# Where keys are normalized and how attention is spread over the projections: a diffusion block on one core

## The chip, the cores and the metric

The kernel runs on one core of one Trainium2 chip. The metric is the device time of one execution in microseconds (us), as the median of several runs. Five engines work side by side, each through its own queue in order: TensorE (PE, matmuls and transposes), VectorE (DVE), ScalarE (ACT), GpSimd (POOL) and SyncE (SP, which issues the DMAs here). Lower is better.

## The reference, cut to what matters

One layer of a transformer block: adaLN from a condition vector, neighbourhood attention over 256 latent tokens and 256 context tokens with 16 heads of 128, and a gated ConvFFN. All in float32.

```python
def project(t):
    q, k, v = jnp.split(t @ w_qkv, 3, axis=-1)
    sh = (t.shape[0], t.shape[1], NA_HEADS, HEAD_DIM)
    return rms_norm(q.reshape(sh), q_g), rms_norm(k.reshape(sh), k_g), v.reshape(sh)

sh1, sc1, g1, sh2, sc2, g2 = adaln(cond_lat, w_ada[i], b_ada[i])
h = modulate(rms_norm(x, norm_mix_g[i]), sh1, sc1)
hc = modulate(rms_norm(ctx, norm_mix_g[i]), csh1, csc1)
q, k, v = project(h)
qc, kc, vc = project(hc)
# per block of 128 queries: scores against 256 latent keys (with a bias and a window) and 256 context keys
p = jax.nn.softmax(jnp.concatenate([s_lat, s_ctx], axis=-1), axis=-1)
o = einsum(p[..., :nk], vb) + einsum(p[..., nk:], vc)
x = x + g1 * (o @ w_o)
hf = modulate(rms_norm(x, norm_ffn_g[i]), sh2, sc2)
x = x + g2 * conv_ffn(hf, ...)
```

What matters here: queries and keys of each head are normalized over the head's 128 features (`rms_norm` with `q_g`, `k_g`), after the projection and before the scores.

## The kernel before, in words

**Split matmuls.** Float32 precision is made of two reduced-precision halves (`F32R`). Each weight tile of 256 x 512 is loaded by SP (`wload`, line 133), ACT casts its high half (`wh`, line 155), and DVE subtracts it from the original for the low half (`wl`, line 156). `ahead` (line 180) makes these pairs two tiles ahead of their use. Activations have high and low halves as well (`hh`, `hl`). A projection (`project`, line 383) adds three products for each weight tile and each tile of 128 tokens (`nat`, lines 378 to 380): six matmuls of 512 columns for one token tile and one weight tile.

**Passes.** The heads are worked in four groups of four (512 columns). A projection pass runs over eight weight tiles; a K or V pass has four token tiles (latent and context tokens), a Q pass two (latent alone). The products of the first K and of V for groups 0 and 1 run ahead, beside the modulation of the input (`first_products`). Then comes a Q pass for group 0, and for g = 0, 1, 2: (V of group 2 when g is 1), K of group g+1, Q of group g+1. After these V of group 3 is projected, then the output projection (`proj` with `w_o`), then the FFN, which fills the span from about 718 us on.

**Side work.** While group g+1 is projected, group g's attention runs in between. It is cut into pieces in a list, `side`; after each token tile of each weight tile `nat` adds `side.rate` to a credit, and each whole credit runs the next piece (line 381). A piece of attention is a score S (three matmuls, bias, maximum, exponential, scaling by the row's sum, line 600), a turn T (four transposes of the probabilities and their split into halves, line 627), or a weighing W (twelve matmuls with V, line 641). A head has two S, two T and one W. The order before is S0 S0 T0 T0 S1 S1 T1 T1 W0 S2 S2 W1 T2 T2 S3 S3 W2 T3 T3 W3, the number being the head's. A second list, `ada`, computes the modulation vectors g1, sh2 and gs2: 12 columns of 8 pieces each and one last piece, 97. Each piece loads 512 KB of `w_ada` (`wa`, three buffers); three pieces of eight multiply and add on DVE (line 279), five multiply on ACT (line 276) and add on POOL (line 277). It is ticked once per weight tile, by 0.44 times the token tiles (line 387).

**Normalization before.** After K and Q of the next group are projected and copied out of PSUM (`out_of_psum`, line 678), the side list is drained, and then `split_k` and `split_q` run `norm_transpose` (line 515) for four and two token tiles. It squares each of the four heads on ACT with an accumulated sum (line 521), forms the mean, takes the inverse root with a power on POOL and one Newton step on DVE (`rsqrt_newton`, lines 195 to 200), multiplies into a new tile `qn` (line 526), transposes it head by head on PE (line 532), and writes the high half with ACT (line 534) and the low half with DVE (line 535). The rows of probabilities, `qn` and some others share three buffers of one tag (`row2k`).

**Who orders the work.** The program is traced in this order, and a scheduler then settles the order of each engine's queue from planned durations: an instruction that stands earlier in the program has precedence among those that are ready, and scores are given a higher precedence. On the chip each engine runs its queue in that order and waits where an operand is late.

Of the kernel before, what the change touches and what calls it, by code (L numbers as in the profile page):

```python
# [15 lines left out]
P = 128  # L16
# [9 lines left out]
CH = 512  # L26
KT = 2

RATE, RATE3 = 0.46, 0.36

WA = 3
EPS = 1e-6
# [18 lines left out]
def block_kernel(  # L51
# [20 lines left out]
    def pj():  # L72
        return ps.tile([P, CH], F32, tag="pj", name="pj", bufs=4)
# [9 lines left out]
    def at():  # L83

        turns.append(0)
        return (ms, mx)[len(turns) % 2]()
# [39 lines left out]


    NDR, REP = 7, 66
    rp = cp.tile([NH * NDR, 31], F32, name="rp")
    nc.scalar.dma_start(rp, rpb)  # L130


    def wload(src, k0, kn, c0, cn, pool=None):
# [201 lines left out]

    xctx = ExitStack()
    xp = xctx.enter_context(tc.tile_pool(name="xp", bufs=1))
    s32 = xp.tile([P, KD, 32], F32, name="s32")
    nc.vector.memset(s32, 0.0)
    nc.scalar.copy(s32[:, :, 0:2], sT)  # L340
# [29 lines left out]
    def nat(psl, tt0, w, kt0, n, first, last):  # L370

        wh, wl = w
        for i, pt in enumerate(psl):
            ts = slice((tt0 + i) * P, (tt0 + i + 1) * P)
            for k in range(n):
                kt = kt0 + k
                a, z = first and k == 0, last and k == n - 1
                nc.tensor.matmul(pt, hh[:, kt, ts], wh[:, k, :], start=a, stop=False)  # L378
                nc.tensor.matmul(pt, hh[:, kt, ts], wl[:, k, :], start=False, stop=False)  # L379
                nc.tensor.matmul(pt, hl(kt, ts), wh[:, k, :], start=False, stop=z)  # L380
# [129 lines left out]
    ap = actx.enter_context(tc.tile_pool(name="ap", bufs=1))  # L510

    def row2k(name):
        return ap.tile([P, CH], F32, tag="r2", name=name, bufs=3)

    def norm_transpose(pt, gcol, dh, dl, t0):

        ss = ap.tile([P, 4], F32, tag="ss", name="ss", bufs=2)
        qn = row2k("qn")
        for h in range(4):
            hc = slice(h * HD, (h + 1) * HD)  # L520
            nc.scalar.activation(qn[:, hc], pt[:, hc], AF.Square, accum_out=ss[:, h : h + 1])
# [4 lines left out]
        nc.vector.tensor_tensor(  # L526
            out=qn.rearrange("p (h d) -> p h d", d=HD), in0=pt.rearrange("p (h d) -> p h d", d=HD),
            in1=r.unsqueeze(2).to_broadcast([P, 4, HD]), op=ALU.mult,
        )
        tp = at()  # L530
        for h in range(4):
            nc.tensor.transpose(tp[:, h * P : (h + 1) * P], qn[:, h * HD : (h + 1) * HD], ident)
        tpv = tp.rearrange("p (h t) -> p h t", t=P)
        nc.scalar.activation(dh[:, :, t0 : t0 + P], tpv, AF.Copy, scale=gcol)
        nc.vector.scalar_tensor_tensor(
            out=dl[:, :, t0 : t0 + P], in0=tpv, scalar=gcol,
            in1=dh[:, :, t0 : t0 + P].bitcast(F32), op0=ALU.mult, op1=ALU.subtract,
        )

    def split_k(kps):  # L540
        kh = kv.tile([P, 4, 2 * T], F32R, tag="kh", name="kh")
        kl = kv.tile([P, 4, 2 * T], F32R, tag="kl", name="kl")
        for tt in range(4):
            norm_transpose(kps[tt], kg, kh, kl, tt * P)
        return kh, kl

    def split_q(qps):
        qq = kv.tile([P, 2, 4, T], F32R, tag="qq", name="qq")
        qh, ql = qq[:, 0], qq[:, 1]
        for tt in range(2):  # L550
            norm_transpose(qps[tt], qg, qh, ql, tt * P)
        return qh, ql
# [36 lines left out]

    def attention(g, q, k, v):  # L590

        (qh, ql), (kh, kl) = q, k

        bank = lambda: ms() if late else at()

        def head(h4):
# [3 lines left out]
            def scores(qt):  # L600
                with tc.high_priority():
                    if qt == 0:
                        if h + 1 < NH:
                            bias(h + 1)
                        st["bt"] = biases.pop(h)
                        st["ph"] = kv.tile([P, 4, T], F32R, tag="pth", name="pth", bufs=2)
                        st["pl"] = ap.tile([P, 4, T], F32R, tag="ptl", name="ptl", bufs=2)
# [11 lines left out]
                    nc.vector.tensor_reduce(out=nm, in_=sp, axis=AX.X, op=ALU.max, negate=True)  # L619
# [4 lines left out]
                    nc.scalar.mul(pr, pr, rs)  # L624
                    st[qt] = pr

            def turn(qt):
                tq = slice(qt * P, (qt + 1) * P)
                pr, tp = st[qt], ms()
                for kt in range(4):  # L630
                    nc.tensor.transpose(
                        tp[:, kt * P : (kt + 1) * P], pr[:, kt * P : (kt + 1) * P], ident
# [23 lines left out]

            return scores, turn, weigh

        heads = [head(h4) for h4 in range(4)]
        s = [[lambda f=h[0], t=t: f(t) for t in range(2)] for h in heads]  # L660
        t = [[lambda f=h[1], t=t: f(t) for t in range(2)] for h in heads]
        w = [[h[2]] for h in heads]
# [5 lines left out]
    cols = [ada_tasks(ap, 2, c, g1T) for c in range(4)]  # L668
    cols += [ada_tasks(ap, 3, c, sh2T) for c in range(4)]
    cols += [ada_tasks(ap, 4, c, gs2T, S_GF) for c in range(4)]  # L670
# [3 lines left out]
    kw, qw = [  # L674
        oT[:, a : a + 2 * n, :].rearrange("p (t a) c -> p t (a c)", t=n) for a, n in ((8, 4), (4, 2))
    ]

    def out_of_psum(pts, dst):

        for tt, pt in enumerate(pts):  # L680
            nc.scalar.copy(dst[:, tt, :], pt)
        return [dst[:, tt, :] for tt in range(len(pts))]

    k = split_k(out_of_psum(kps, kw))
    q = split_q(out_of_psum(project(0, 2), qw))
    for g in range(3):
        side.extend(sum(attention(g, q, k, v), []))
        c0 = (g + 1) * CH
        side.rate = RATE3 if g == 1 else RATE
        if g == 1:  # L690
            v = [split_v(project(2 * D + c0, 4), g + 1)]
        if g == 2:
            kq = big.tile([P, 6, CH], F32, tag="row1", name="kq")
            kw, qw = kq[:, :4], kq[:, 4:]
# [9 lines left out]
    v = []  # L704
    early, rest = attention(3, q, k, v)
# [45 lines left out]
    sacc2 = ap.tile([P, T], F32, name="sacc2")  # L751
    tail = [sacc2]

    def omv(kt, c):
        return om[0][:, kt, c]
# [7 lines left out]
    for i, pieces in enumerate(WO):  # L763
# [3 lines left out]
        elif i > 1:  # L767
            pts = {c: [bank() for _ in range(cn // P)] for c, cn, _, _ in pieces}
        for c, cn, k_lo, k_hi in pieces:
            tick = (lambda: side.tick(cn / 340)) if i == 0 else (lambda: ada.tick(1.0))  # L770
            proj(w_o, NH, c, cn, omv, tick, k_lo, k_hi, pts[c], fold)
        if i == 0:
            side.drain()
            continue
        if i == len(WO) - 2:
            ada.drain()
# [182 lines left out]
```

## Time and profile before

| what | value |
|---|---|
| median of 3 runs | 1447.01 us (1440.1 to 1449.32) |
| the profiled execution's own time | 1445.85 us |
| its span, first to last instruction | 1444.0 us |
| granted TensorE clock, mean | 0.992 |
| PE / DVE / ACT / POOL busy | 1399.1 / 1000.0 / 778.5 / 281.1 us |
| HBM read | 312.75 MB, 219 GB/s over the span |

Busy time is the sum over an engine's instructions without their overlap; matmuls are pipelined, so a new one starts every 0.23 us while one of 512 columns is shown as lasting 0.39. A row of a group names the line, engine, operation, tiles written and read, shapes and count, then busy us and mean ns of one, then the engine's idle time just before and what ended it. A row of a window has each engine's busy us (and its number of instructions), the granted clock as a share, the DMA engines' share and GB/s. A row of waits has the total, the number of times and the longest. A row of a line's own view has minimum, median and maximum ns, and the first and last start.

### The profile page before, as it was taken

To read this page: it belongs to the slowest core of one execution; us is meant where nothing else is said; L and a number is where in the kernel's file an instruction comes from. 1 tells how busy PE (TensorE), PEld (TensorE's weight loads), DVE (VectorE), ACT (ScalarE), POOL (GpSimd) and SP (SyncE) were. 2 spreads that over 40 slices of the span, in tenths; PEclk is the share of its full clock that TensorE was granted. 3 is DMA by queue.
4 is the path that set the end of the run, shared out by engine and by line. 5 is a ranking of instruction groups with operands and counts; after the bars stand their busy time and mean duration, and the time that the engine had idled before them with its cause. 6 is when DMAs were issued, how large, how long until landed. Compare 5 with 4: busy or idle time off the path is not lost.

```text
span 1444.0 us, 21091 instructions
## 1 busy us (share of the span) xinstructions
PE 1399.1 (97%) x7608; PEld 1167.8 (81%) x7608; DVE 1000.0 (69%) x1541; ACT 778.5 (54%) x1356; POOL 281.1 (19%) x208
## 2 busy tenths in 40 slices
PE   5999999999999999999899999999999999999998
PEld 2666787877787887888788888888888888888888
DVE  4556687686868768756768787887877775545454
ACT  4322265775555675755556566665666654333333
POOL 1000025465445555300101111111111000000000
PEclk9999999999999999999899999999999999999999
DMA  9999548687677677545567777777776666566554
GB/s 308 357 333 313 190 125 269 206 259 218 214 219 254 215 239 232 178 138 189 174 201 224 237 230 242 236 229 234 228 240 196 182 175 206 182 207 204 172 173 156
DMA packets 208920, 317.14 MB, mean 220 GB/s; under 512 B 23360, under 2 KB 87744, under 8 KB 208816
## 3 DMA queue, kind: packets, MB, share of 16 engines
q1 hardware_dynamic: 208688, 315.79, 70.4%
q8 instruction: 59, 0.97, 0.3%
q14 instruction: 45, 0.37, 0.1%
q10 hardware_dynamic: 128, 0.01, 0.0%
HBM read 312.75 MB, written 3.01 MB: 219 GB/s over the span
## 4 chain that ended last, share of the span: by engine, by line
PE 74%; issue 9%; DMA 5%; DVE 4%; ACT 3%; POOL 2%; SPq 1%; DVEq 0%; POOLq 0%; ACTq 0%
PE pj L727 18%; PE pj L733 9%; PE mx L727 8%; PE ms L727 7%; PE pj L379 5%; PE pj L378 5%; PE pj L380 5%; PE mx L733 4%; PE ms L733 4%; DMA wa<-in_w_ada 3%; PE ms L411 2%; PE mx L378 2%; PE mx L379 2%; PE mx L380 2%; POOL acc L277 2%
## 5 line engine op out<-in xcount | busy, mean ns | idle before, releaser
L156 DVE TENSOR_TENSOR wl<-wr,wh 128x1024 fp32r<-128x1024 f32 (+2 forms) x425 | 503.8, 1186 | 280.6 <-PE pj L733 106.3
L155 ACT CAST wh<-wr 128x1024 fp32r<-128x1024 f32 (+2 forms) x425 | 412.1, 971 | 428.8 <-PE pj L727 135.1
L277 POOL TENSOR_TENSOR acc<-acc,wa 128x512 f32<-128x512 f32 x144 | 223.6, 1553 | 428.8 <-issue 260.1
L379 PE MATMUL pj<-wl,hh 128*128 128x512 f32 x512 | 204.7, 400 | 3.5 <-DVE wl L156 3.4
L380 PE MATMUL pj<-wh,hl 128*128 128x512 f32 x512 | 201.7, 397 | 0.0
L378 PE MATMUL pj<-wh,hh 128*128 128x512 f32 x512 | 194.4, 400 | 2.5 <-ACT hh L450 2.5
L727 PE MATMUL pj<-hf,wh 128*128 128x512 f32 x688 | 176.3, 396 | 2.0 <-DVE hf L819 2.0
L727 PEld LDWEIGHTS pj<-hf,wh 128*128 128x128 f32 x688 | 124.9, 191 | 25.1 <-DVE hf L819 2.8
L276 ACT ACTIVATE wa<-wa,sT 128x512 f32<-128x512 f32 x144 | 97.4, 718 | 74.5 <-DMA wa<-in_w_ada 69.3
L379 PEld LDWEIGHTS pj<-wl,hh 128*128 128x128 f32 x512 | 97.7, 191 | 27.2 <-DVE wl L156 6.3
L378 PEld LDWEIGHTS pj<-wh,hh 128*128 128x128 f32 x512 | 96.8, 190 | 26.9 <-issue 3.4
L380 PEld LDWEIGHTS pj<-wh,hl 128*128 128x128 f32 x512 | 97.5, 191 | 19.5
L733 PEld LDWEIGHTS pj<-hf,wl 128*128 128x128 f32 x688 | 94.6, 192 | 6.8
L733 PE MATMUL pj<-hf,wl 128*128 128x256 f32 x688 | 97.8, 285 | 0.0
L727 PE MATMUL mx<-hf,wh 128*128 128x512 f32 x352 | 97.7, 394 | 0.0
L727 PE MATMUL ms<-hf,wh 128*128 128x512 f32 x336 | 90.9, 390 | 0.0
L279 DVE SCALAR_TENSOR_TENSOR acc<-wa,sT,acc 128x512 f32<-128x512 f32 x80 | 73.7, 921 | 6.9 <-DMA wa<-in_w_ada 6.3
L727 PEld LDWEIGHTS ms<-hf,wh 128*128 128x128 f32 x336 | 63.1, 188 | 14.2
L727 PEld LDWEIGHTS mx<-hf,wh 128*128 128x128 f32 x352 | 60.6, 190 | 7.8
L478 DVE TENSOR_TENSOR vsum<-vsum,mx 128x512 f32<-128x512 f32 x64 | 43.2, 684 | 34.2 <-PE mx L380 34.0
L733 PEld LDWEIGHTS mx<-hf,wl 128*128 128x128 f32 x352 | 53.7, 189 | 7.1 <-DVE wl L156 0.4
L584 POOL TENSOR_TENSOR bt<-bt,maskt 128x384 f32<-128x384 f32 x16 | 17.9, 1123 | 206.4 <-DMA bt<-rpd 173.7
(251 smaller groups left out, 2212.0 us busy)
## 6 DMA issues: line engine op xcount, KB each, us to landing
wr<-in_w_up SPq DMA_DIRECT2D x160, 512.0 KB, 4.5
wa<-in_w_ada SPq DMA_DIRECT2D x128, 512.0 KB, 4.6
wr<-in_w_qkv SPq DMA_DIRECT2D x93, 512.0 KB, 4.8
wr<-in_w_down SPq DMA_DIRECT2D x63, 512.0 KB, 4.8
wx<-in_w_ada SPq DMA_DIRECT2D x56, 512.0 KB, 8.6
wr<-in_w_o SPq DMA_DIRECT2D x24, 512.0 KB, 3.9
wr<-in_w_down SPq DMA_DIRECT2D x45, 256.0 KB, 3.0
wr<-in_w_up SPq DMA_DIRECT2D x16, 384.0 KB, 3.4
```

The lines of the kernel that those rows point to most:

```text
L155: a = nc.scalar.copy(hi[:, :kn, :cn], w[:, :kn, :cn])
L156: b = nc.vector.tensor_tensor(out=lo[:, :kn, :cn], in0=w[:, :kn, :cn], in1=hi[:, :kn, :cn].bitcast(F32), op=ALU.subtract,)
L276: nc.scalar.mul(w[:, k, :], w[:, k, :], s)
L277: nc.gpsimd.tensor_add(acc, acc, w[:, k, :])
L279: nc.vector.scalar_tensor_tensor(out=acc, in0=w[:, k, :], scalar=s, in1=acc, op0=ALU.mult, op1=ALU.add)
L378: nc.tensor.matmul(pt, hh[:, kt, ts], wh[:, k, :], start=a, stop=False)
L379: nc.tensor.matmul(pt, hh[:, kt, ts], wl[:, k, :], start=False, stop=False)
L380: nc.tensor.matmul(pt, hl(kt, ts), wh[:, k, :], start=False, stop=z)
L411: nc.tensor.matmul(ap_[32 * k : 32 * k + 32, :n], s32[:, 4 * q + k, :], w[:, k * n : (k + 1) * n], start=(q == 0), stop=(q == 3), tile_pos ...
L478: nc.vector.tensor_add(acc[:, h0 + i, :], acc[:, h0 + i, :], pr_[i])
L727: nc.tensor.matmul(pts[b][:, : t1 - t0], wh[:, k, bs], mov(kt, slice(t0, t1)), start=(kt == 0 and t0 == 0), stop=False,)
L733: nc.tensor.matmul(pts[b][:, :T], wl[:, k, bs], mov(kt, slice(0, T)), start=False, stop=(kt == kn - 1),)
```

## The change

- **Keys and queries are normalized in place.** `norm` squares all four heads with one ACT instruction, sums with one DVE reduction, and multiplies into the tile that it read. It runs inside `out_of_psum`, so K's normalization stands in the program after the K projection and ahead of the Q projection.
- **The transposes become pieces.** `flips` makes one piece per token tile: four transposes and the writing of the halves. K's four and Q's two go to the head of the next pass's side list. The first K's go into the first Q pass.
- **Rates.** The side list is spread evenly over a pass: (pieces + 0.5)/48 per token tile, /80 for g = 1, and 16.5/32 for the V pass of group 3. `ada` is ticked per token tile, by 0.5 in K and V passes and 0.1 in Q passes; what is left runs in the output projection at 0.6 a tick instead of 1.0. Its columns come in the order g1, gs2, sh2.
- **Attention** has the order S00 S01 S10 S11 T00 T01 S20 T10 T11 S21 W0 T20 S30 W1 T21 S31 W2 T30 T31 W3 (head, then half). T takes its bank from both tags. The row buffers become four; Q's copies out of PSUM use them too.
- `rp` and `sacc2` lie in other pools, and `rp`'s load stands a little later in the program.

```diff
-RATE, RATE3 = 0.46, 0.36
+ADA_RATE = {2: 0.1, 4: 0.5}
...
             side.tick(side.rate)
+            ada.tick(ada.rate)
 
     def project(c0, nt):
         psl = [pj() for _ in range(nt)]
+        ada.rate = ADA_RATE[nt]
         for kt in range(0, KD, KT):
             nat(psl, 0, weight(w_qkv, kt, KT, c0, CH), kt, KT, kt == 0, kt == KD - KT)
-            ada.tick(0.44 * nt)
+        ada.rate = 0.0
         return psl
...
-        return ap.tile([P, CH], F32, tag="r2", name=name, bufs=3)
+        return ap.tile([P, CH], F32, tag="r2", name=name, bufs=4)
-
-    def norm_transpose(pt, gcol, dh, dl, t0):
+    def norm(pt):
+
+        sq = row2k("sq")
+        nc.scalar.activation(sq, pt, AF.Square)
         ss = ap.tile([P, 4], F32, tag="ss", name="ss", bufs=2)
-        qn = row2k("qn")
-        for h in range(4):
-            hc = slice(h * HD, (h + 1) * HD)
-            nc.scalar.activation(qn[:, hc], pt[:, hc], AF.Square, accum_out=ss[:, h : h + 1])
+        nc.vector.tensor_reduce(
+            out=ss, in_=sq.rearrange("p (h d) -> p h d", d=HD), axis=AX.X, op=ALU.add
+        )
...
+        pv = pt.rearrange("p (h d) -> p h d", d=HD)
         nc.vector.tensor_tensor(
...
+            out=pv, in0=pv, in1=r.unsqueeze(2).to_broadcast([P, 4, HD]), op=ALU.mult
+        )
+
+    def flips(src, gcol, slots):
+
+        st = []
+
+        def flip(tt):
+            if not tt:
+                st.extend(slots())
+            tok = slice(tt * P, (tt + 1) * P)
+            tp = at()
+            for h in range(4):
+                nc.tensor.transpose(
+                    tp[:, h * P : (h + 1) * P], src[tt][:, h * HD : (h + 1) * HD], ident
+                )
+            tpv = tp.rearrange("p (h t) -> p h t", t=P)
+            nc.scalar.activation(st[0][:, :, tok], tpv, AF.Copy, scale=gcol)
+            nc.vector.scalar_tensor_tensor(
+                out=st[1][:, :, tok], in0=tpv, scalar=gcol, in1=st[0][:, :, tok].bitcast(F32),
+                op0=ALU.mult, op1=ALU.subtract,
+            )
+
+        return [lambda tt=tt: flip(tt) for tt in range(len(src))], st
...
-                pr, tp = st[qt], ms()
+                if qt == 0:
+                    st["ph"] = kv.tile([P, 4, T], F32R, tag="pth", name="pth", bufs=2)
+                    st["pl"] = ap.tile([P, 4, T], F32R, tag="ptl", name="ptl", bufs=2)
+                pr, tp = st[qt], bank()
...
-        seq = s[0] + t[0] + s[1] + t[1]
         if g == 3:
-            return [seq, w[0] + s[2] + t[2] + w[1] + s[3] + w[2] + t[3] + w[3]]
-        return [seq + w[0] + s[2] + w[1] + t[2] + s[3] + w[2] + t[3] + w[3]]
+            return [
+                order("S00 S01 S10 S11 T00 T01 S20 T10 T11 S21"),
+                order("W0 T20 S30 W1 T21 S31 W2 T30 T31 W3"),
+            ]
+        return [
+            order("S00 S01 S10 S11 T00 T01 S20 T10 T11 S21 W0 T20 S30 W1 T21 S31 W2 T30 T31 W3")
+        ]
...
+    def out_of_psum(pts, dst=None):
+
+        out = [dst[:, tt, :] if dst is not None else row2k("qw") for tt in range(len(pts))]
+        for o, pt in zip(out, pts):
+            nc.scalar.copy(o, pt)
+        for o in out:
+            norm(o)
+        return out
...
+    kf, k = flips(out_of_psum(kps, kw), kg, k_slots)
+    side.extend(kf)
+    side.rate = 0.3
+    qs = out_of_psum(project(0, 2))
+    side.drain()
+    kf = []
     for g in range(3):
-        side.extend(sum(attention(g, q, k, v), []))
+        qf, q = flips(qs, qg, q_slots)
+        pieces = kf + qf + sum(attention(g, q, k, v), [])
         c0 = (g + 1) * CH
-        side.rate = RATE3 if g == 1 else RATE
+        side.extend(pieces)
+        side.rate = (len(pieces) + 0.5) / (80 if g == 1 else 48)
...
-        kps = out_of_psum(project(D + c0, 4), kw)
-        qps = project(c0, 2)
-        if g != 1:
-            qps = out_of_psum(qps, qw)
+        ks = out_of_psum(project(D + c0, 4), kw)
+        kf, k = flips(ks, kg, k_slots)
+        qs = out_of_psum(project(c0, 2))
         side.drain()
-        k = split_k(kps)
-        q = split_q(qps)
...
-    side.extend(early)
-    side.rate = RATE3
-    vps = project(2 * D + c0, 4)
+    side.extend(kf + qf + early)
+    side.rate = 16.5 / 32
+    vps = project(2 * D + 3 * CH, 4)
...
-            tick = (lambda: side.tick(cn / 340)) if i == 0 else (lambda: ada.tick(1.0))
+            tick = (lambda: side.tick(cn / 400)) if i == 0 else (lambda: ada.tick(0.6))
```

More of the change, by code (lines that the diff above doesn't have):

```diff
@@ L337, in block_kernel @@
     xp = xctx.enter_context(tc.tile_pool(name="xp", bufs=1))
+    rp = xp.tile([NH * NDR, 31], F32, name="rp")
+    nc.scalar.dma_start(rp, rpb)
     s32 = xp.tile([P, KD, 32], F32, name="s32")
@@ L525, in norm_transpose, with k_slots, q_slots @@
         r = rsqrt_newton(ap, ss, 4, "n")
+        pv = pt.rearrange("p (h d) -> p h d", d=HD)
         nc.vector.tensor_tensor(
-            out=qn.rearrange("p (h d) -> p h d", d=HD), in0=pt.rearrange("p (h d) -> p h d", d=HD),
-            in1=r.unsqueeze(2).to_broadcast([P, 4, HD]), op=ALU.mult,
-        )
[L530 to L547, printed above, removed]
+            out=pv, in0=pv, in1=r.unsqueeze(2).to_broadcast([P, 4, HD]), op=ALU.mult
+        )
+    def flips(src, gcol, slots):
[16 more added lines that the diff above has]
+        return [lambda tt=tt: flip(tt) for tt in range(len(src))], st
+    def k_slots():
+        return [kv.tile([P, 4, 2 * T], F32R, tag=tag, name=tag) for tag in ("kh", "kl")]
+    def q_slots():
         qq = kv.tile([P, 2, 4, T], F32R, tag="qq", name="qq")
[L549 to L552, printed above, removed]
+        return qq[:, 0], qq[:, 1]
     def split_v(vps, g):
@@ L590, in attention @@
     def attention(g, q, k, v):
-        (qh, ql), (kh, kl) = q, k
         bank = lambda: ms() if late else at()
@@ L605, in scores @@
                         st["bt"] = biases.pop(h)
-                        st["ph"] = kv.tile([P, 4, T], F32R, tag="pth", name="pth", bufs=2)
-                        st["pl"] = ap.tile([P, 4, T], F32R, tag="ptl", name="ptl", bufs=2)
+                    (qh, ql), (kh, kl) = q, k
                     tq = slice(qt * P, (qt + 1) * P)
@@ L657, in head @@
             return scores, turn, weigh
[L659 to L662, printed above, removed]
-        seq = s[0] + t[0] + s[1] + t[1]
-        if g == 3:
-            return [seq, w[0] + s[2] + t[2] + w[1] + s[3] + w[2] + t[3] + w[3]]
-        return [seq + w[0] + s[2] + w[1] + t[2] + s[3] + w[2] + t[3] + w[3]]
+        heads = [dict(zip("STW", head(h4))) for h4 in range(4)]
@@ new lines, in order @@
+        def order(names):
+            return [
+                lambda f=heads[int(n[1])][n[0]], t=[int(x) for x in n[2:]]: f(*t)
+                for n in names.split()
+            ]
+        if g == 3:
+            return [
+                order("S00 S01 S10 S11 T00 T01 S20 T10 T11 S21"),
+                order("W0 T20 S30 W1 T21 S31 W2 T30 T31 W3"),
+            ]
+        return [
+            order("S00 S01 S10 S11 T00 T01 S20 T10 T11 S21 W0 T20 S30 W1 T21 S31 W2 T30 T31 W3")
+        ]
@@ L668, in block_kernel @@
     cols = [ada_tasks(ap, 2, c, g1T) for c in range(4)]
+    cols += [ada_tasks(ap, 4, c, gs2T, S_GF) for c in range(4)]
     cols += [ada_tasks(ap, 3, c, sh2T) for c in range(4)]
-    cols += [ada_tasks(ap, 4, c, gs2T, S_GF) for c in range(4)]
     ada.extend(ada_pieces(cols))
     v, v1 = [[split_v([vsums[g][:, tt, :] for tt in range(4)], g)] for g in range(2)]
[L674 to L682, printed above, removed]
@@ L773, in block_kernel @@
             side.drain()
+            sacc2 = kv.tile([P, 4, 2 * T], F32, tag="kl", name="sacc2")[:, 0, :T]
+            tail = [sacc2]
             continue
```

11 lines of the change are left out of this document (3 added, 8 removed).

## Prediction

> **What bounds the kernel now.** First the page: who is busy.
>
> ```profile
> span 1444.0 us, 21091 instructions
> ...
> PE 1399.1 (97%) x7608; PEld 1167.8 (81%) x7608; DVE 1000.0 (69%) x1541; ACT 778.5 (54%) x1356; POOL 281.1 (19%) x208
> ...
> L156 DVE TENSOR_TENSOR wl<-wr,wh 128x1024 fp32r<-128x1024 f32 (+2 forms) x425 | 503.8, 1186 | 280.6 <-PE pj L733 106.3
> ...
> L277 POOL TENSOR_TENSOR acc<-acc,wa 128x512 f32<-128x512 f32 x144 | 223.6, 1553 | 428.8 <-issue 260.1
> ...
> L279 DVE SCALAR_TENSOR_TENSOR acc<-wa,sT,acc 128x512 f32<-128x512 f32 x80 | 73.7, 921 | 6.9 <-DMA wa<-in_w_ada 6.3
> ```
>
> PE is busy 97% of the span, and the diff neither adds nor removes a matmul or a transpose. So the change can win only what PE stands idle or slow in the stages that it touches: the projections with attention beside them, from about 200 to 605 us. Second view, the busy times by window; I cut it where PE's transposes of normalized tiles (L532) stand, the seams between one group's passes and the next: 309 to 328, 431 to 471 and 533 to 571.
>
> ```profile
> core 0: us, PE busy (x) PEld busy (x) DVE busy (x) ACT busy (x) POOL busy (x), PEclk, DMA share, GB/s
> 200.00:226.00 26.00, 25.53 (x116) 20.08 (x114) 24.64 (x31) 17.14 (x24) 11.07 (x7) 1.00 0.65 206
> 226.00:244.00 18.00, 17.46 (x81) 14.36 (x82) 12.92 (x22) 11.05 (x29) 9.11 (x7) 1.00 0.79 270
> 244.00:309.00 65.00, 64.02 (x317) 52.89 (x315) 45.18 (x64) 42.73 (x84) 32.17 (x23) 1.00 0.76 237
> 309.00:328.00 19.00, 14.54 (x78) 11.60 (x77) 17.72 (x32) 14.31 (x48) 14.35 (x11) 1.00 0.76 232
> 328.00:431.00 103.00, 100.22 (x489) 82.87 (x488) 73.61 (x103) 58.76 (x111) 47.02 (x36) 1.00 0.71 219
> 431.00:471.00 40.00, 36.81 (x158) 29.28 (x157) 32.76 (x52) 22.75 (x53) 21.39 (x14) 0.91 0.73 237
> 471.00:533.00 62.00, 62.00 (x311) 51.91 (x310) 45.29 (x66) 43.24 (x85) 32.83 (x23) 1.00 0.79 244
> 533.00:571.00 38.00, 35.09 (x165) 28.45 (x164) 30.59 (x55) 23.83 (x60) 23.94 (x17) 0.96 0.69 215
> 571.00:605.00 34.00, 33.19 (x165) 27.55 (x164) 23.27 (x45) 21.99 (x43) 13.97 (x10) 1.00 0.72 216
> 605.00:704.00 99.00, 96.95 (x597) 86.05 (x596) 64.14 (x106) 51.59 (x86) 0.00 (x0) 1.00 0.49 157
> ...
> 200.00:605.00 405.00, 388.85 (x1867) 318.99 (x1866) 305.98 (x464) 255.80 (x533) 205.85 (x142) 0.99 0.73 229
> ```
>
> From 200 to 605 PE is idle for 405.00 - 388.85 = 16.2 us. Of it the three seams hold 4.46 + 3.19 + 2.91 = 10.6, the attention stretches 244 to 309 and 328 to 431 hold 0.98 + 2.78 = 3.8, the first Q pass (200 to 244) 1.0, and the last stretch 0.8. Besides, the granted clock falls at two seams: 40 x 0.09 + 38 x 0.04 = 5.1 us of PE work lost. DVE is 93% busy in the first seam (17.72 of 19). Third view: what PE waited for between 200 and 610 us.
>
> ```profile
> PE pj L379 <- DVE wl L156: 3.4, 4, 1.5
> PE ms L532 <- DVE qn L526: 2.7, 2, 1.5
> PE mx L532 <- DVE qn L526: 2.5, 2, 1.7
> PE mx L645 <- ACT pth L635: 2.1, 1, 2.1
> PE ms L631 <- ACT pr L624: 1.4, 2, 0.8
> PE ms L532 <- ACT kh L534: 1.3, 1, 1.3
> PE ms L532 <- DVE gs2T L291: 0.8, 1, 0.8
> ```
>
> The transposes at L532 wait for the normalized tile (L526), and for a bank that kh's eviction still holds (L534). Matmuls wait for a low half of the weights (L156) that DVE made late. L631 and L645 are attention's transposes and products, which wait for the piece shortly before them. Fourth, the timeline of the worst seam:
>
> ```profile
> 449.64 0.63 PE L532 MATMUL ms<-ident,qn 128*128 128x128 f32 x4 [1.14 <-DVE qn L526]
> 451.76 0.79 PE L379 MATMUL pj<-wl,hh 128*128 128x512 f32 x1 [1.50 <-DVE wl L156]
> 452.36 0.63 PE L380 MATMUL pj<-wh,hl 128*128 128x512 f32 x1
> 452.78 0.63 PE L378 MATMUL pj<-wh,hh 128*128 128x512 f32 x1
> ...
> 458.17 0.40 PE L380 MATMUL pj<-wh,hl 128*128 128x512 f32 x1
> 458.40 0.39 PE L378 MATMUL pj<-wh,hh 128*128 128x512 f32 x1
> ```
>
> After the two waits matmuls start 0.42 us apart instead of 0.23. The first one after a wait also takes 0.60 to the next, 0.18 more than its neighbours: about 0.18 us of refill that no idle column shows, for some 15 waits 2.7 us. So the most that can come back is 16.2 + 5.1 + 2.7 = 24.0 us.
>
> **The change, part by part.**
>
> Seams. Now all six normalizations of a group come after both projections in program order, and their transposes ahead of the next pass. After the change K's are normalized behind the K projection, so during the Q pass; and all six transposes are spread over the next pass as the first pieces of its side work: at (26 + 0.5)/48 pieces per token tile of 6 matmuls (6 x 0.23 = 1.4 us), one every 2.5 us. K's tiles are then ready some 20 us before they are used. Q's first flip stands behind four of K's, 12 us into the pass; in the first group, with none of K's ahead, at 4 us, the one place where a chain can still be late. The seams hold 10.6 + 5.1 + 7 waits x 0.18 (1.3) = 17.0; I leave 2.5 for that place and for weights still late: **-14.5**. Bounds: -17.0, and 0 if the chains are late all the same.
>
> Attention. A score (S) and its transposes (T) now lie four or five pieces apart, the last head's second one three, with four row buffers instead of three. This covers the waits at L631. T1 to W1 grows likewise; T31 to W3 stays one piece, so a wait of the kind at L645 can stay. 3.8 + 5 x 0.18 = 4.7; I leave 1.7: **-3.0** (0 to -4.7).
>
> First Q pass. The ada rate there falls from 0.88 pieces a weight tile to 0.2. The 1.0 + 0.4 us belong to late low halves on a DVE that is 24.64 of 26 busy: **-0.7** (0 to -1.4).
>
> Squares. Four squares with accumulated sums become one square and a reduction on DVE:
>
> ```profile
> L521 ACT ACTIVATE qn<-oT 128x128 f32<-128x128 f32 x64 | 19.0, 301 | 0.7 <-DVE nt L197 0.5
> ...
> L521 ACT ACTIVATION_READ_ACCUMULATOR qn<-oT 128x1 f32 x64 | 12.2, 191 | 0.0
> ...
> L360 ACT ACTIVATE sq<-xc 128x512 f32<-128x512 f32 x8 | 4.7, 622 | 1.4 <-DMA xc<-in_ctxT 1.4
> ```
>
> ```profile
> L619 DVE TENSOR_REDUCE nm<-ms 128x1 f32<-128x512 f32 x18 | 12.4, 688 | 0.4
> L526 DVE TENSOR_TENSOR qn<-oT,nr 128x512 f32<-128x512 f32 x16 | 11.0, 688 | 0.3
> ...
> L196 DVE TENSOR_TENSOR nt<-nr 128x4 f32<-128x4 f32 x24 | 10.3, 429 | 8.3 <-POOL nr L195 8.3
> ```
>
> ACT saves 4 x (0.30 + 0.19) - 0.62 = 1.3 us a tile, 32 us over 24 tiles, behind PE. DVE gets 0.69 more per tile (a reduction of 512 elements, L619), 16.5 us over the stage's 405, of which 306 are busy: behind PE as an average, but not in the Q pass, where K's four now lie. The multiply in place costs what L526 cost.
>
> Q pass on DVE. It lasts 96 matmuls x 0.23 = 22 us. In it fall 8 splits x 1.19 = 9.5; four normalizations, each 0.69 + 0.69 and four small operations; ada, 1.6 pieces of 0.58 (73.7 us of L279 over 128 pieces), 0.9; and about nine attention pieces, some 5 us at the 0.69 of L619 or less. The small operations:
>
> ```profile
> L196 DVE TENSOR_TENSOR nt<-nr x24: 144/156/1257, 189.1 to 563.4; 128x4 f32<-128x4 f32 x24
> ```
>
> Between 0.156 (median) and 0.429 (mean; the long ones reach 1.257), so a normalization is 2.0 to 3.1 us, and the pass 23 to 28 of 22: 1 to 6 over, over three passes 3 to 18, less two splits made ahead of each (2.4 each): 0 to 11. What stands against it is what the same pass carried before:
>
> ```profile
> 430.50:452.50 22.00, 21.24 (x33) 0.97 0.73 236
> ```
>
> 21.24 of 22 on DVE, with K's normalizations and kl evictions and seven ada pieces, and PE waited there mostly for transposes put in its queue too soon. Five of seven ada pieces leave, and their POOL additions with them. I take **+1.5** (0 to +11).
>
> Row buffers. The new squares and Q's copies take the four buffers that the score rows use. Where K is normalized at most three rows stand in wait of their transposes, so one is free; if none were, the square would hold ACT until the next transposes, 2.5 us, with the weights' casts (L155) behind it and PE behind them. **0** (0 to +2.5 in each of three passes).
>
> ada. 97 pieces. The new rates run 5 x 32 x 0.5 = 80 in K and V passes and 4 x 16 x 0.1 = 6 in Q passes; 11 are left for the output projection, at 0.6 a tick. There DVE has 99 - 64 us free and POOL all of it, and PE's 97 us of matmuls cover the pieces. Two column ends fall there, each with transposes that can wait as the one behind gs2T did (0.8): **+0.7** (0 to +2). In K and V passes pieces come every 2.7 us instead of 3.1; costed at nothing behind PE, priced as a rival below. The rp load that moves, and the smaller ticks of the last group, are nothing: neither stands on PE's path.
>
> Sum: 14.5 + 3.0 + 0.7 - 1.5 - 0.7 = 16.0 us. The profiled execution took 1445.85 us (span 1444.0): 1445.85 - 16.0 = 1429.85. The median of the runs, 1447.01, is 1.2 above it, so **1431**.
>
> **The rivals.**
>
> Q passes bound by DVE. K's normalizations stand ahead of the Q pass's splits in program order, so a full DVE makes weights late. For it: 21.24 of 22 before. Against it: less ada and POOL beside it. At the upper bound 11 instead of 1.5: 1431 + 9.5 = 1441.
>
> The clock. It may fall by itself, not through these waits; then 5.1 us stay: 1436. For it: 309 to 328 has the longest idle time and a clock of 1.00. Against it: the half pace above begins right behind two waits. The Trainium skill (TensorE: Matmul & The Clock Gate, What's actually happening) ties the slow clock to an idle window of about 3.4 us; here the waits are 1.14 and 1.50, so by that rule they would not be the cause and the sum would be this 1436; the trace speaks against the rule as far as these rows go.
>
> The other side: K and V passes bound by POOL. 16 ada pieces a pass (44 us) are 18 additions, and some three more come for the bias:
>
> ```profile
> L277 POOL TENSOR_TENSOR acc<-acc,wa x144: 1267/1318/2722, 212.2 to 1109.6; 128x512 f32<-128x512 f32 x144
> ```
>
> ```profile
> SPq L139 <- POOL acc L277: 141.1, 69, 5.8
> ```
>
> At the mean, 1.55, 21 of them take 33 us. From 44/21 = 2.1 us each POOL is full. SP's queue, which already waits behind additions for 141 us (5.8 at the longest), then holds the next weights behind an ada load that waits for its buffer, and PE starves. At 2.3 they take 48 of 44 us: 4.3 x 5 passes = 21, so 1431 + 21 = 1452. For it: additions reach 2.72, and denser pieces meet more of DVE's splits. Against it: half of them take 1.32 or less, and the mean must grow by 35% for 14% more pieces before anything is late. The Trainium skill (SBUF — State Buffer, Who interferes with whom) has the later of two such operations wait for all of the earlier, so every addition behind a split would be a long one; the trace has long ones, as many as lift the mean above the median.
>
> It doesn't do what it says: order on each engine is settled from planned times, and the new chains may be misplaced as the old were; the waits move and stay: 1446.
>
> **How the numbers follow.** Forecast 0.6, its own range 1424 to 1437; DVE 0.13; clock 0.1; POOL 0.1; nothing 0.07. What a measurement tells from no change is 1%, 14.5 us, so faster means under 1432.5. The forecast's case lies there in three quarters: 0.6 x 0.75 = 0.45 faster; the rest of it and 1436, 1441 and 1446 are within 1%: 0.15 + 0.3 = 0.45; POOL 0.10 slower. The range goes from 1422 (24 of 24 us back is 1423) to 1447, past all cases but POOL's.
>
> **What would show it.** Right: from 200 to 605 PE idle falls from 16 to about 5 us, the clock is 1.00 at the seams, no transpose of normalized tiles waits over 0.5 us, and DVE in Q passes is full but low halves are late by under 1 us. Wrong: matmuls that wait for L156's splits inside Q passes (DVE), half pace without a wait ahead (clock), a POOL addition over 2.1 us in the mean with weight loads behind it (POOL), or the same sum of waits under other names.

## The result, and the profile after

| | before | changed |
|---|---|---|
| median, first measurement | 1446.15 us | 1433.43 us |
| ratio, with its 95% interval | | 0.9919 [0.9894, 0.9943] |
| the same two kernels, second measurement | 1447.60 us | 1433.43 us |
| ratio | | 0.9906 [0.9886, 0.9926] |
| span of the profiled executions | 1444.0 us | 1433.7 and 1430.0 us |

The change makes the kernel 13 to 14 us faster, 0.8 to 0.9%. The forecast was 1431. First the page of the changed kernel: the split is now line 154 and POOL's addition line 275.

```profile
PE 1398.5 (98%) x7608; PEld 1169.1 (82%) x7608; DVE 1004.2 (70%) x1565; ACT 766.2 (53%) x1190; POOL 276.8 (19%) x208
...
L154 DVE TENSOR_TENSOR wl<-wr,wh 128x1024 fp32r<-128x1024 f32 (+2 forms) x425 | 501.6, 1181 | 286.1 <-PE pj L756 93.6
...
L275 POOL TENSOR_TENSOR acc<-acc,wa 128x512 f32<-128x512 f32 x144 | 218.5, 1518 | 560.2 <-issue 243.0
```

PE does the same work in 10.3 us less. Then the busy times by window. The stretch from 200 us to the first matmuls of the output projection ends at 596 instead of 605. The places of the three seams of before are now the ends of the Q passes, at about 315, 446 and 534; they lie in the windows 303 to 330, 419 to 460 and 503 to 580.

```profile
core 0: us, PE busy (x) PEld busy (x) DVE busy (x) ACT busy (x) POOL busy (x), PEclk, DMA share, GB/s
200.00:244.00 44.00, 43.80 (x199) 35.91 (x198) 34.28 (x48) 24.20 (x32) 12.16 (x9) 1.00 0.61 185
244.00:303.00 59.00, 56.83 (x289) 47.06 (x288) 48.39 (x87) 40.30 (x68) 27.43 (x21) 1.00 0.73 224
303.00:330.00 27.00, 27.00 (x133) 22.52 (x132) 20.80 (x26) 15.63 (x23) 12.38 (x10) 1.00 0.68 216
330.00:419.00 89.00, 89.00 (x429) 73.87 (x428) 65.16 (x99) 53.98 (x87) 46.85 (x35) 1.00 0.82 257
419.00:460.00 41.00, 41.00 (x205) 34.36 (x205) 27.65 (x45) 22.23 (x33) 14.81 (x11) 1.00 0.57 170
460.00:503.00 43.00, 42.73 (x208) 34.43 (x207) 35.66 (x61) 27.69 (x49) 20.69 (x14) 1.00 0.83 256
503.00:535.00 32.00, 29.86 (x152) 24.93 (x151) 21.91 (x40) 20.83 (x35) 15.96 (x12) 0.95 0.58 173
535.00:580.00 45.00, 45.00 (x217) 37.17 (x216) 34.78 (x57) 25.70 (x41) 21.60 (x16) 1.00 0.83 273
580.00:596.00 16.00, 14.25 (x59) 11.16 (x58) 14.62 (x25) 12.40 (x27) 7.06 (x5) 0.79 0.65 206
596.00:693.00 97.00, 96.07 (x595) 85.54 (x593) 73.32 (x109) 55.39 (x91) 21.44 (x11) 1.00 0.59 195
200.00:596.00 396.00, 389.48 (x1876) 321.41 (x1875) 303.26 (x481) 242.95 (x391) 178.95 (x131) 0.99 0.72 225
```

At all three seams PE no longer stands idle, and the clock is 1.00: 27.00 of 27, 41.00 of 41, and behind the third 45.00 of 45. From 200 to 596 it is idle for 396.00 - 389.48 = 6.5 us, against 16.2 before. What is left stands at three places: 2.2 us in the first attention stretch (244 to 303), 2.1 in the third Q pass (503 to 535), and 1.75 between the V pass of group 3 and the output projection (580 to 596). The granted clock fell at the last two: 32 x 0.05 + 16 x 0.21 = 5.0 us lost, as much as before, though elsewhere. So the account of this profile is 9.6 us less idle, 0.1 us of clock, and five or so waits less to refill after (0.9): 10.6 us, against 10.3 in the span. The waits of PE in that stretch have new names:

```profile
PE pj L379 <- DVE wl L154: 2.3, 2, 2.1
PE ms L616 <- DVE ptl L645: 1.7, 1, 1.7
PE ms L658 <- DVE vv L568: 1.1, 2, 0.7
PE ms L654 <- ACT vv L567: 0.5, 2, 0.3
```

No wait for a normalized tile is among them (the transposes are line 544 now). L379 waits for a low half that DVE made late, L616 (a score) stands behind a turn whose low half is late, and L658 and L654 are products that wait for the halves of V. The turn ahead of L616 is late because ACT, which makes its high half, had been held by an `ada` piece: the load of `wa` took 5.91 us and landed at 269.9, ACT's two multiplications followed to 271.3, and only then came the turn's cast.

### The profile page after: what moved, and what is told of

It reads as the page before. It is cut to its first block, busy times and chain, and to the rows that moved or that the text cites. A ratio compares the mean times of both kernels' runs of the same rounds, so it can differ in the third digit from the quotient of the medians.

```text
span 1433.7 us, 20944 instructions
## 1 busy us (share of the span) xinstructions
PE 1398.5 (98%) x7608; PEld 1169.1 (82%) x7608; DVE 1004.2 (70%) x1565; ACT 766.2 (53%) x1190; POOL 276.8 (19%) x208
## 4 chain that ended last, share of the span: by engine, by line
PE 80%; DMA 7%; DVE 4%; POOL 3%; issue 2%; ACT 2%; SPq 1%; DVEq 0%; POOLq 0%; ACTq 0%
PE pj L750 20%; PE pj L756 10%; PE mx L750 9%; PE ms L750 7%; DMA wa<-in_w_ada 5%; PE pj L379 5%; PE pj L378 5%; PE pj L380 5%; PE mx L756 5%; PE ms L756 4%; POOL acc L275 2%; PE ms L413 2%; PE mx L378 2%; PE mx L379 2%; PE mx L380 2%
## 5 line engine op out<-in xcount | busy, mean ns | idle before, releaser
L275 POOL TENSOR_TENSOR acc<-acc,wa 128x512 f32<-128x512 f32 x144 | 218.5, 1518 | 560.2 <-issue 243.0
L379 PE MATMUL pj<-wl,hh 128*128 128x512 f32 x512 | 204.2, 399 | 2.3 <-DVE wl L154 2.3
L379 PEld LDWEIGHTS pj<-wl,hh 128*128 128x128 f32 x512 | 97.2, 190 | 23.4 <-DVE wl L154 3.5
L277 DVE SCALAR_TENSOR_TENSOR acc<-wa,sT,acc 128x512 f32<-128x512 f32 x80 | 70.2, 877 | 7.2 <-DMA wa<-in_w_ada 6.6
L756 PE MATMUL mx<-hf,wl 128*128 128x256 f32 x352 | 55.9, 282 | 0.0
```

The source lines that it names most:

```text
L275: nc.gpsimd.tensor_add(acc, acc, w[:, k, :])
L277: nc.vector.scalar_tensor_tensor(out=acc, in0=w[:, k, :], scalar=s, in1=acc, op0=ALU.mult, op1=ALU.add)
L756: nc.tensor.matmul(pts[b][:, :T], wl[:, k, bs], mov(kt, slice(0, T)), start=False, stop=(kt == kn - 1),)
```

## The experiments

Every ratio is to the kernel before, measured on the same chip; the changed kernel itself stands at 0.9919 and 0.9906. A thousandth is 1.45 us. The intervals are some 2 to 3 us wide to either side, so differences of that size between two altered kernels are not certain.

**The seams put back.** `norm` and the flips of a group run between its passes again, tile by tile, by a helper `seam`. The side list's rates follow from the pieces that are left; everything else stays as changed.

```diff
-        for o in out:
-            norm(o)
...
+        k = seam(ks, kg, k_slots)
+        q = seam(qs, qg, q_slots)
```

> The changed kernel with the normalizations and transposes of a group put back between its passes; order of attention, ada rates and the one square stay as changed. Theory that the seams carry the gain: about 12 to 15 us of the gain are lost, 1443 to 1448 us, and the transposes wait for normalized tiles again. Rival that the thin ada rate in Q passes carries it: the seams then cost little, 1434 to 1438.

Measured: 1447.64 us, ratio 1.0012 [0.9995, 1.0030]. All of the gain is lost, 0.0093 to 0.0106 or 13 to 15 us against the two measurements of the unaltered kernel, and the waits for normalized tiles are back:

```profile
PE ms L544 <- DVE qw L530: 2.0, 2, 1.7
...
PE ms L544 <- DVE kw L530: 1.9, 1, 1.9
```

So the new ada rate, the new order and the one square bring nothing without the move of the normalizations.

**The seams alone.** The old order of attention, 0.44 ada pieces per token tile in every pass, four squares with sums. The move stays, and small things with it (the banks of the turns, the fourth row buffer, the order of ada's columns).

> The changed kernel with the old order of attention, the old mean ada rate of 0.44 pieces per token tile in every pass and four squares with sums; only the early normalization and the transposes as pieces are left of the change. Theory (seams): 1430 to 1436. Rival (ada rate): DVE, ACT and POOL are too full in Q passes for the keys' normalizations, and it stands at 1440 to 1450.

Measured: 1441.28 us, 0.9958 [0.9940, 0.9975]. That is inside the rival's range, at its lower end: the move alone brings 5 to 6 us, less than half. PE's waits for low halves are 7.2 us up to 600 us, against 2.3.

**The flat ada rate.**

```diff
-ADA_RATE = {2: 0.1, 4: 0.5}
+ADA_RATE = {2: 0.44, 4: 0.44}
```

> The changed kernel with 0.44 ada pieces per token tile in every pass, so 0.88 per weight tile in Q passes. Theory (seams): up to 3 us slower than the changed kernel, 1433 to 1437, low halves a little later in Q passes. Rival (ada rate): 5 to 15 us slower, 1438 to 1448.

Measured: 1442.87 us, 0.9974 [0.9956, 0.9991]. This one number costs 0.0055 to 0.0068 or 8 to 10 us, as the rival said. The first row of PE's waits says where:

```profile
PE pj L379 <- DVE wl L154: 11.1, 11, 3.4
```

The waits for normalized tiles do not come back; matmuls of the passes wait for low halves instead, 11.1 us against 2.3, and all eleven waits stand in Q passes. Now that the keys' normalizations stand in the Q pass ahead of its splits, ada's work there makes the weights late: in the last three Q passes, from the copy of K's last tile to that of Q's, DVE is busy for 88.2 of 97.8 us here, and for 61.3 of 87.9 in the changed kernel.

This kernel is no faster than the one above with the seams alone, 1441.28, on the same chip. So at the flat rate the new order of attention and the one square bring nothing either.

**The old order of attention.** The last group, which these lines do not show, goes back as well: eight of its pieces run in the V pass instead of ten, at the rates that belong to them.

```diff
-order("S00 S01 S10 S11 T00 T01 S20 T10 T11 S21 W0 T20 S30 W1 T21 S31 W2 T30 T31 W3")
+order("S00 S01 T00 T01 S10 S11 T10 T11 W0 S20 S21 W1 T20 T21 S30 S31 W2 T30 T31 W3")
```

> The changed kernel with the old order of attention, scores right ahead of their transposes. Theory: 3 us slower by the waits of transposes and products for probabilities, 1435 to 1438. Rival that the scheduler sets the distances whatever the order of the pieces: 1432 to 1435.

Measured: 1437.82 us, 0.9943 [0.9919, 0.9968], 3.5 us slower than the first measurement of the changed kernel and 5.4 than the second, inside the theory's range. Its interval overlaps with both of theirs, so the size is not certain. Waits of turns and products return:

```profile
PE ms L640 <- ACT pr L630: 3.0, 1, 3.0
...
PE mx L657 <- DVE ptl L645: 1.4, 1, 1.4
```

The longest of them, 3.0 us, does not stand in an attention stretch but at the last seam, at 589.3, where this kernel divides the last group's pieces at another place.

**Four squares on ACT.** `norm` with the squares and accumulated sums of before.

> The changed kernel with four squares and accumulated sums on ACT instead of one square and a reduction on DVE. Theory that DVE is the tight engine in Q passes: 1 to 3 us faster than the changed kernel, 1430 to 1433, though ACT has 1.3 us more for each of 24 tiles. Rival that ACT's longer chain delays the casts of weights: 1 to 4 us slower, 1434 to 1438.

Measured: 1435.47 us, 0.9912 [0.9898, 0.9926]. In microseconds that lies in the rival's range, but the kernel before took 1447.25 on this chip, and by the ratio there is no difference from the changed kernel that this measurement shows. Its trace leaves room for a small cost: from 200 to 597 us PE is idle for 10.1 us, against 6.5 and 6.9 up to the same place in the unaltered kernel's two profiles, and less clock is lost than in the first of them. A microsecond or two either way is not excluded.

**Where W0 waits.** The second measurement of the unaltered kernel stood beside this and the next two.

> The changed kernel unaltered, as the yardstick of this chip. All theories: 1430 to 1437, 0.99 of the kernel before.

```diff
-order("W0 T20 S30 W1 T21 S31 W2 T30 T31 W3"),
+order("T20 S30 W0 T21 S31 W1 W2 T30 T31 W3"),
```

> The changed kernel with the last group's order behind the V pass begun with T20 and S30 instead of W0, so that the first product with V stands two pieces later. Theory that about 5 us between the V pass and the output projection are lost because W0 waits for V's halves: 3 to 5 us faster than the changed kernel, 1428 to 1431. Rival that the place only shifts to the split of the earlier heads' output (om), which the output projection needs in any case: within 1 us of the changed kernel.

Measured: 1436.76 us, 0.9921 [0.9903, 0.9940]. My theory fell. The rival's mechanism shows, though its number missed: the kernel is 2 to 3 us slower than the unaltered one beside it, not within 1. W0 out of the way, PE waits for the first halves of the earlier heads' output, which queue on DVE behind V's: the output projection starts 5.5 us after the pass's last matmul, against 5.8 and 5.3 in the unaltered kernel's two profiles. From its timeline, at the end of the V pass:

```profile
586.32 0.60 PE L640 MATMUL ms<-ident,pr 128*128 128x128 f32 x4
587.76 0.50 PE L616 MATMUL ms<-kh,qq 128*128 128x512 f32 x1 [0.84 <-ACT pr L628]
...
591.63 1.65 PE L750 MATMUL pj<-om,wh 128*128 128x512 f32 x3 [2.90 <-DVE om L575]
```

**Which of ada's engines it is.** Two kernels with the flat rate: one without POOL's additions of the attention stage, one without DVE's multiply-adds.

```diff
-                    nc.gpsimd.tensor_add(acc, acc, w[:, k, :])
+                    if i == 5:
+                        nc.gpsimd.tensor_add(acc, acc, w[:, k, :])
```

```diff
-                else:
+                elif i == 5:
                     nc.vector.scalar_tensor_tensor(
```

> 0.44 ada pieces per token tile in every pass, with POOL's additions of the attention stage's ada columns left out (so g1, sh2 and gs2 lack those parts). Theory that POOL is what hurts in Q passes (DVE's operations stretch beside additions, and the inverse roots queue behind them): the waits for low halves fall from 11 to under 4 us and the time to 1430 to 1436. Rival that DVE's own ada work fills it: it stays at 1440 to 1444.

> 0.44 ada pieces per token tile in every pass, with DVE's multiply-adds of the attention stage's ada columns left out (so g1, sh2 and gs2 lack those parts); POOL's stay. Theory that POOL is what hurts: 1438 to 1444. Rival that DVE's own load is what hurts: 1430 to 1436, waits for low halves under 4 us.

Measured: 1419.21 us, 0.9802 [0.9780, 0.9823], without the additions, and 1423.79 us, 0.9835 [0.9813, 0.9857], without the multiply-adds. I had expected one of the two to matter; either is enough, and both gain about twice what I gave them. With either left out the kernel is faster than the changed one too; `ada` also stands behind waits that the thin rate leaves, as the turn ahead of L616 showed. With the flat rate and everything in place the low halves' row was 11.1; without the additions, in the windows up to 580 us, PE waits for almost nothing:

```profile
PE pj L751 <- DVE om L576: 0.4, 1, 0.4
PE pj L380 <- DVE wl L154: 0.2, 1, 0.2
```

The splits between 200 and 590 us, with the additions and then without:

```profile
L154 DVE TENSOR_TENSOR wl<-wr,wh 128x1024 fp32r<-128x1024 f32 x71 | 97.7, 1378 | 17.0 <-PE pj L379 7.8 <-DMA wr<-in_w_qkv 6.1 <-issue 2.9
L277 DVE SCALAR_TENSOR_TENSOR acc<-wa,sT,acc 128x512 f32<-128x512 f32 x60 | 55.4, 923 | 3.4 <-DMA wa<-in_w_ada 2.7
```

```profile
L154 DVE TENSOR_TENSOR wl<-wr,wh 128x1024 fp32r<-128x1024 f32 x77 | 93.9, 1222 | 36.7 <-PE pj L380 31.8 <-issue 2.7 <-ACT oT L663 0.8
L278 DVE SCALAR_TENSOR_TENSOR acc<-wa,sT,acc 128x512 f32<-128x512 f32 x60 | 46.7, 778 | 1.1 <-DMA wa<-in_w_ada 0.4
```

A split takes 1.38 us beside the additions and 1.22 without; a multiply-add 0.92 and 0.78. DVE then waits for PE (31.8 us) and no longer the reverse. The additions also hold ada's buffers: ACT's waits for ada's loads fall from 56.2 to 31.1 us without them. The kernel without multiply-adds settles a part of this. Its splits are as long as ever:

```profile
L154 DVE TENSOR_TENSOR wl<-wr,wh 128x1024 fp32r<-128x1024 f32 x74 | 104.0, 1405 | 23.1 <-PE pj L379 16.2 <-issue 4.4 <-ACT wa L274 2.4
```

Yet PE waits for low halves only 1.6 us up to 600. So longer splits alone do not do the harm. Nor do the inverse roots alone, which queue behind additions: DVE waits for them 7.6 us with everything in place and 7.3 without the multiply-adds. What both kernels share is a DVE with room in the Q passes. In the last three of them, bounded as above, it is busy for:

| kernel | DVE busy, us | of | PE waits for low halves up to 600 us |
|---|---|---|---|
| flat rate | 88.2 | 97.8 (90%) | 11.1 |
| flat rate, no additions | 74.1 | 86.2 (86%) | 0.2 |
| flat rate, no multiply-adds | 75.3 | 95.8 (79%) | 1.6 |
| changed kernel | 61.3 | 87.9 (70%) | 2.3 |

The multiply-adds load DVE directly, the additions by what they add to each split and multiply-add beside them. In both kernels ACT's waits for ada's loads fall too (to 40.0 without the multiply-adds), and how much of the gain is due to that stays open.

**The changed kernel without the additions.**

> The changed kernel with POOL's additions of the attention stage's ada columns left out (so g1, sh2 and gs2 lack those parts). Theory that the ada rate matters through what its additions do to DVE and to the buffers: 1416 to 1422, the same as with 0.44 pieces in every pass and no additions. Rival that the thin rate in Q passes is worth something beside that: 1409 to 1415.

Measured: 1420.50 us, 0.9811 [0.9798, 0.9824], the same as with the flat rate within the intervals. Without the additions the thin rate brings nothing that this measurement shows: its worth is bound to them.

**A quiet end of the V pass.** No ada pieces in the last two weight tiles of group 3's V pass, and the four pieces moved to the output projection at 0.8 a tick. This came from ACT's timeline of the changed kernel (the pass's last matmul starts at 585.8):

```profile
581.32 1.34 ACT L274 ACTIVATE wa<-wa,sT 128x512 f32<-128x512 f32 x2 [2.48 <-DMA wa<-in_w_ada]
...
584.64 1.34 ACT L274 ACTIVATE wa<-wa,sT 128x512 f32<-128x512 f32 x2 [0.57 <-DMA wa<-in_w_ada]
585.89 0.56 ACT L567 CAST vv<-pj 128x512 fp32r<-128x512 f32 x1
```

ACT waits for ada's load, and V's first cast stands behind it.

> The changed kernel with no ada pieces in the last two weight tiles of the V pass of group 3; the four pieces go to the output projection, at 0.8 a tick. Theory that ACT, waiting there for an ada load, makes V's halves and so the output projection late: the first matmul of the output projection starts 2 to 3 us after the last one of the V pass instead of 6, 2 to 4 us faster, 1429 to 1432. Rival that the splits of V and of the earlier heads' output take this time anyway: within 1 us of the changed kernel.

Measured: 1438.48 us, 0.9936 [0.9921, 0.9951]. The place behaved as the theory said: the first V cast starts at 581.4, and the output projection starts 1.9 us after the pass's last matmul (587.46 after 585.56), not 6; PE is busy for 17.00 of 17 us from 580 to 597, at a clock of 1.00. Yet the kernel comes out slower than the unaltered one, by 0.0017 to 0.0030 or 2.5 to 4 us, with intervals that overlap, because the output projection now pays. Its window here, and in the unaltered kernel's second profile:

```profile
587.50:697.00 109.50, 102.16 (x609) 89.18 (x609) 83.24 (x123) 63.24 (x107) 30.45 (x17) 0.98 0.59 195
```

```profile
590.00:689.00 99.00, 98.53 (x610) 87.86 (x609) 77.50 (x121) 59.07 (x100) 21.03 (x11) 1.00 0.60 196
```

PE idles 7.3 us there instead of 0.5, and the clock of 0.98 takes another 2.2. POOL has 17 operations instead of 11, and the low halves are late again:

```profile
PE pj L758 <- DVE wl L154: 3.2, 2, 2.4
PE ms L758 <- DVE wl L154: 2.3, 2, 1.4
```

**The same, and no ada in Q passes**, 1.1 a tick in the output projection.

> As the kernel without ada pieces in the last two weight tiles, and with none in Q passes either; the output projection takes 1.1 a tick. Theory that the late low halves left in Q passes come from ada's remains: 1 to 2 us faster than without the second edit, 1427 to 1431. Rival that they come from the normalizations' own waits for POOL's inverse roots: no difference between the two.

Measured: 1449.29 us, 1.0016 [1.0006, 1.0026], 16 us slower than the changed kernel. The longest wait behind the first 200 us of all these traces stands in the output projection: a column of ada that PE is to transpose, and whose sum is not there yet.

```profile
PE ms L286 <- DVE acc L283: 10.3, 1, 10.3
```

This kernel does not answer the question about Q passes. Its waits for low halves are nearly gone there, 0.2 us up to 600 against 2.5, but so is the reason for them that the changed kernel's trace gives (next section): POOL is free when the inverse roots come. It shows only that the output projection takes 0.6 pieces a tick and not 1.1.

## Why the prediction was right, and where it was not

The forecast was 1431 and the measurement 1433.4, inside the range; the gain of 0.8 to 0.9% lies just under the 1% that I had put as the bound of "faster". Step by step:

- **Seams, -14.5: right in size, but not by itself.** At their places idle time and clock came back in full. With the rest of the change in place they are worth 13 to 15 us; with the old rate, order and squares 5 to 6. I had sized the ada rate as a step of its own at 0.7 us in the first Q pass, and named its effect on the other Q passes in one sentence under +1.5. The runs show it to be the condition of the whole step: 8 to 10 us. My rival "Q passes bound by DVE" (up to 11 us) is what happens without it, with 11.1 us of waits for low halves. The parts do not add up: taken out one at a time, seams, rate and order cost more than the whole change brings, so each is worth this much only with the others there.
- **Attention, -3.0: half of it or less shows in the traces.** PE's idle time in the attention stretches was 3.8 us and is 2.4 and 2.9 in the two profiles of the changed kernel (244 to 303, 330 to 419, 460 to 503). The old order put back costs 3.5 to 5.4 us, but with much of its waiting at the last seam, and at the flat rate, together with the squares, it costs nothing.
- **First Q pass, -0.7: right.** PE's idle time from 200 to 244 fell from 1.0 to 0.2; with the flat rate it is 2.2.
- **Squares: right** as far as the measurement goes; no difference was seen, and a microsecond or two would not have been.
- **Q passes on DVE, +1.5: the late weights came, by another mechanism, and the size is off.** One Q pass of three shows them, with 2.1 us of wait and 1.6 of clock. It was no overload: DVE is busy for 21.91 of 32 us there. My working had 23 to 28 us of DVE in a pass of 22. The 22 left out that attention's matmuls run on PE in the same pass: from copy to copy group 1's Q pass (286.75 to 315.22) lasts 28.5 us with PE never idle, and DVE is busy for 20.3 of them. The late split sat behind one small operation:

```profile
501.80 1.23 DVE L154 TENSOR_TENSOR wl<-wr,wh 128x1024 fp32r<-128x1024 f32 x1
505.48 0.16 DVE L194 TENSOR_TENSOR nt<-nr 128x4 f32<-128x4 f32 x1 [2.45 <-POOL nr L193]
...
508.97 1.21 DVE L154 TENSOR_TENSOR wl<-wr,wh 128x1024 fp32r<-128x1024 f32 x1
```

The Newton step (L194) waits in DVE's queue for POOL's inverse root, and the split behind it in the queue comes late. POOL was not busy with additions at that time:

```profile
503.44 1.03 POOL L593 TENSOR_TENSOR bt<-bt,maskt 128x384 f32<-128x384 f32 x1 [7.89 <-DMA bt<-rpd]
504.42 2.01 POOL L193 TENSOR_TENSOR nr<-ss,mhalf 128x4 f32<-128x4 f32 x2
```

It stood idle for 7.89 us until the load of a head's bias for attention had landed; the mask (L593) and then the inverse roots (L193) followed in its queue, though DVE had their input ready at 501.9. A sum of busy times could not show that.

- **The last seam: failed.** I had left its 0.8 us as it was. It grew to 1.75 us of idle and, in one profile of two, 3.4 of clock, because ada's pieces now run to the end of the V pass. Before, they had just ended there. The kernel with a quiet end shows the cause: without the pieces PE does not wait there at all.
- **ada in the output projection, +0.7: it cost nothing** (PE idle 0.9 us of 97, 2.0 of 99 before), but only at this rate: a third more per tick brought 7 us more of idle time.
- **The clock: right at the three seams, wrong as a gain.** It is 1.00 at the seams, but 5.0 us were lost to it in the first profile, as much as before, and 1.6 in the second: the falls moved to new waits. In the second profile the third Q pass is slow again and the last seam is not:

```profile
503.00:535.00 32.00, 30.00 (x151) 25.00 (x150) 22.66 (x40) 21.19 (x35) 15.96 (x12) 0.95 0.61 177
...
580.00:595.00 15.00, 13.26 (x68) 10.47 (x67) 12.76 (x24) 11.07 (x25) 6.28 (x4) 1.00 0.67 211
```

The rival "the clock falls by itself" is not borne out: in both profiles each fall stands behind waits, though a wait does not always bring one (last section).

- **POOL as the bound: did not come.** An addition takes 1.52 us in the mean, 1.55 before.

So the number is in part luck. The seams and the output projection gave more than I had put down; attention, the third Q pass and the last seam gave less, and these errors offset each other in good part.

What stays open is how much of ada's harm in Q passes comes by DVE's load and how much by the buffers that its pieces hold.

## What to carry to other kernels

When a chain is moved from a seam into a pass, the load of that pass is part of the move's price: empty it first, and test the move with and without the emptying. When the length of a pass is estimated, count all that its engine does in it, the side work too. Look at what each waiting instruction has queued behind it on its own engine, not at busy shares alone. Background work that is moved away from one full place arrives at another; here three places (Q passes, the end of the V pass, the output projection) traded the same few pieces.

## What the runs showed of the hardware

Half pace can come after a wait of about 2 us. In the changed kernel's second profile:

```profile
509.44 0.50 PE L379 MATMUL pj<-wl,hh 128*128 128x512 f32 x1 [2.00 <-DVE wl L154]
509.78 0.53 PE L380 MATMUL pj<-wh,hl 128*128 128x512 f32 x1
510.11 0.63 PE L378 MATMUL pj<-wh,hh 128*128 128x512 f32 x1
510.53 0.63 PE L616 MATMUL ms<-kh,qq 128*128 128x512 f32 x1
```

A wait of 2.00 us, and from the third matmul on they start 0.42 us apart instead of 0.23. The Trainium skill (TensorE: Matmul & The Clock Gate, What's actually happening) ties the slow clock to an idle window of about 3.4 us. Here it fell after less, and the row decides. But such a wait does not bring it every time. In the kernel with the quiet end the same matmul at the same place waits 2.33 us (to 510.19), from the second on the next ones start 0.23 to 0.27 us apart, and the granted clock from 503 to 535 is 1.00. What decides is not shown. At the last seam nearly the same waits brought the fall in one profile (0.79) and not in the other (1.00): that is 3.4 us, most of the 3.7 between the two spans.
